# A two-layer encoder trunk: small vectors, turned weights, scores, states and sums of squares put elsewhere

## The chip, the core and the metric

The kernel runs on one core of a Trainium2 chip. Its time is the device time of one execution in microseconds (us). Five engines work side by side, each through its own queue in order: PE (matrix products; its weight loads are listed as PEld), DVE (vector work), ACT (activation functions and copies), POOL (GpSimd) and SP (here it only issues DMAs). PE writes to PSUM, eight banks of 128 x 512 float32; the tags `mm`, `sm`, `lg` and `tp` own two banks each.

## What is computed

Input `x` is 512 tokens by 1024, `mem` 256 tokens by 1024. Cut to what matters:

```python
for i in range(2):
    h = rms_norm(x, attn_norm[i])
    if i == 0:   # differential attention: 6 heads, two softmaxes each, T5 bias
        mix = diff_attention(q, k, v, qk_norm, lambdas, out_norm, rel_bias, lam_init)
    else:        # gated linear attention: 4 heads, chunks of 64
        mix = gla_attention(q, k, v, r, gate_low, gate_w, gate_b, out_norm)
    cross = memory_cross_attention(mem_q, mem, mem_norm[i], w_mem_kv[i], mem_qk_norm[i])
    x = x + concat([mix, cross]) @ w_out[i]
    x = x + conv_ffn(rms_norm(x, ffn_norm[i]), w_up[i], conv_w[i], conv_b[i], w_down[i])

# in gla_attention, per chunk, with eg = exp(cumulated gate), ieg = 1/eg:
a_past   = (q * eg)  @ (k * ieg).T
a_future = (q * ieg) @ (k * eg).T
scores   = where(key <= query, a_past, a_future)
# the state over the chunks: state = decay * state + (k * exp(g_end - g)).T @ v
```

## The kernel before

The residual stream is kept transposed: eight tiles `xT[k]` of 128 channels by 512 tokens. Large products are done in three parts: an operand is split into a rounded high half and a low half (`xh`, `xl`), so are the weights (`whi`, `wlo`), and high times high, high times low and low times high are summed in PSUM. Weights come from memory in pieces (`load_raw`, issued by SP); ACT casts the high half (L199), DVE subtracts for the low half (L200). Splitting an activation is one ACT instruction (L232) and one DVE instruction (L233). The token norm is applied after the product, by a scale per token worked out from sums of squares: `squares` squares a tile on ACT (L332) and adds it to the running sum on DVE (L334); `token_rsqrt` sums over the channels by products with ones (L340).

PE's order is that of the program. The other engines' order is chosen by a scheduler with a model of the times, save in the opening (the block over `ini`), where ACT, DVE, POOL and SP also keep the program's order among the instructions of that block; instructions from outside may be put between them. In the opening the first weight piece and the tiles of x are split, k by k, while PE multiplies them; at k = 4 two rows of biases are made (`bias_rows`, L314 and L315); at k = 6 the second piece is split and the token scale is made. Behind it come loads of constants: `cols` (the norm gains as columns) and `lv` (four lambda vectors). `small_vectors` multiplies seven of these columns by fixed factors (L414 to L417) and works out lambda (L320 to L323).

While a stage waits for softmaxes and the like, PE is given other products from a queue (`Filler`): `fill(us)` takes some us of units from it, `need(name)` takes all up to a mark.

Memory attention (`MemAttn`) goes in slots: `logits` of a block (L484, row maxima on DVE L487, exponentials on ACT L491), `turn` (four transposes into a `tp` bank, L168, copied out by L501), `values` (L513). In layer 0 its slots lie between those of the differential heads (L601 scores, L606 bias and maxima, L637 values) and share the `tp` banks with `prepare` and `finish`.

Gated attention has four heads. `products(h)` makes the scaled q and k, six DVE instructions (L832 to L837). `scores(h)` makes the past scores of two blocks at a time (L843, evicted by a masked copy on DVE, L845, and a copy on ACT, L848), then the future scores of all four (L851, evicted by L852). Each of these three takes one `lg` bank. `states(h, b2)` makes the chunk states (L870); the first is copied by DVE (L873), the others are added to the decayed state (L875).

`update(n, p, gain, acc)` adds a product to `xT[n]` (L946), splits the sum and takes its squares. It is called by the output projection (`out_proj`, tiles of 3 to 6 products of 3 parts each, bank tag `mm`) and by the down-projections of the MLP (`ffn`). The MLP's scale per token is made by `row_scales` (L1002) after the first up-projection.

Of the kernel before, what the change touches and what calls it, by code (L numbers as in the profile page):

```python
# [127 lines left out]
def trunk(ctx, tc, x_t, mem_t, wpack, cols_a_d, cols_d, conv_d, gate_d, rel_bias, diff_lambda, consts, onehot, out):  # L128
# [200 lines left out]

    def squares(src, acc):  # L330
        sq = xtile()
        A.activation(sq, src, AF.Square)  # L332
        if acc[0] is not None:
            V.tensor_add(sq, sq, acc[0])  # L334
        acc[0] = sq

    def token_rsqrt(tag, sq, nb, y, on_dve=False):
        p = bank(tag)
        for b in range(nb):
            mm(p[:, b:b + 1], sq[:, blk(b)], ones[:, 0:1], start=True, stop=True)  # L340
        return rsqrt(p[:, :nb], nb, 1.0 / D, on_dve, y=y)

    E = mybir.EngineType
    load = nc.sync.dma_start
    with tc.tile_pool(name="ini", bufs=1) as ip, tc.manual_schedule(engines={E.Activation, E.DVE, E.Pool, E.SP}):
# [20 lines left out]
        load(oh, onehot)  # L366
        second = [load_raw(raw_tile(), WTILE) for _ in range(3)]
        parts, acc, split_w = [], [None], [None]
        made.append(parts)
# [13 lines left out]
        for k in range(KT):  # L383
            if k + 1 < KT:
                operands(k + 1)
            if k == 0:
                second.append(load_raw(raws[0], WTILE))
            if k == 4:
                bias_rows(rb, oh, bs)
            if k == KT - 2:  # L390
                make_piece(second)
                weights(("qk", 0))
                token_rsqrt("lg", acc[0], NB, r_x[:, 0])
                for c in range(2):
                    load(bias_d[:, 512 * c:min(512 * c + 512, 640)], bs[c])
            hi, lo = parts[k]
            for b in range(NB):
                mm(first[b], xh[k][:, blk(b)], hi, start=k == 0, stop=False)
                mm(first[b], xh[k][:, blk(b)], lo, start=False, stop=False)
                mm(first[b], xl[k][:, blk(b)], hi, start=False, stop=k == KT - 1)  # L400

    load(C[:, 0:640], consts[:, 0:640])
    for i in range(4):
        load(memT[i], mem_t[i])
    load(cols, cols_d)
    load(lv, diff_lambda[0].rearrange("a b -> (a b)").partition_broadcast(128))
    for l in range(2):
        load(cv[l].rearrange("p a b -> p (a b)"), conv_d[l])
    load(gw, gate_d)

    def small_vectors():
        lam(lv, xtile()[:, 0:128].rearrange("p (a b) -> p a b", a=2))
        for c in (c_dq, c_mq(0), c_mq(1)):
            V.tensor_scalar_mul(c, c, 0.125)  # L414
        V.tensor_scalar_mul(c_do, c_do, 1.0 - LAM_INIT)
        for t in range(3):
            V.tensor_scalar_mul(c_go(t), c_go(t), 0.5)  # L417

# [42 lines left out]
    class MemAttn:  # L461
# [33 lines left out]
        def turn(self, u):  # L495
            pe, sm = self.live[u]
            pt = bank("tp")
            for t in range(4):
                transpose(pt[:, blk(t)], pe[:, blk(t)])
            pT = xtile()  # L500
            A.copy(pT, pt)  # L501
            self.live[u] = pT, sm
# [39 lines left out]
    def diff_layer(pool, mix):  # L542
# [117 lines left out]
        norms(0, 1)  # L660
        small_vectors()
        gemm(xh, xl, NB, ("vm", 0), 512, halves(v0, qm))
# [52 lines left out]
    def gla_layer(pool, mix, acc):  # L715
# [106 lines left out]
        def products(h):  # L822
# [7 lines left out]
            x = qx[h] = pool.tile([96, NB, 192], F32, name="qx", bufs=2)  # L830
            x = x.rearrange("p b (c n) -> p b c n", n=64)
            V.tensor_mul(x[:, :, 0:3:2], pq[:96].rearrange("p (b c n) -> p b c n", b=NB, c=2), eg)  # L832
            V.tensor_mul(ki, pk[:96], ie)
            V.tensor_mul(qi, pq[:96], ie)
            V.tensor_mul(x[:, :, 1], x[:, :, 2], eg[:, :, 0, 63:64].to_broadcast([96, NB, 64]))
            V.tensor_mul(ke, pk[:96], egs[h % 2])
            V.tensor_mul(ed, pk[:96], ed)  # L837

        def scores(h):
            for b2 in range(2):  # L840
                pp = bank("lg")
# [6 lines left out]
                A.copy(sv[0:64, 2 * b2:2 * b2 + 2, 64:128], pv[0:64, :, 1])  # L848
            pp = bank("lg")
            for b in range(NB):  # L850
                mm(pp[:, blk(b)], ke[:, blk(b)], qi[:, blk(b)], start=True, stop=True)  # L851
            V.copy_predicated(sv, MF.unsqueeze(1).to_broadcast([128, NB, 128]),  # L852
                              pp.rearrange("p (b n) -> p b n", b=NB))

# [9 lines left out]
        def states(h, b2):  # L864
            if h:
                F.need("v")
            p = bank("lg")
            for b in (0, 1) if b2 == 0 else (2,):
                sl = p[:96, blk(b % 2, 192)]
                mm(sl, kd[h][:, b], v[:, b, blk(h, 192)], start=True, stop=True)  # L870
                sn = pool.tile([96, 192], F32, name="st", bufs=4)
# [72 lines left out]

    def update(n, p, gain, acc):
        V.tensor_add(xT[n], xT[n], p)  # L946
# [3 lines left out]
        split(xh[n], xl[n], xT[n], gain(n))  # L950
        squares(xT[n], acc)

# [7 lines left out]
    def out_proj(l, mix, part, acc):  # L960
        got = {}

        def unit(c, ks, n, i):
# [6 lines left out]
            if i == len(ks) - 1:  # L970
                update(2 * c + n, p, None if acc is None else (lambda k: c_ffn(l, k)), acc)
        todo, kk = tiles(l, part)
# [4 lines left out]
    def ffn(pool, l, acc):  # L977
# [32 lines left out]
        for half, nq in enumerate(HALVES):  # L1010
# [22 lines left out]
            for c in range(4):  # L1033
# [4 lines left out]
                for n in range(2):  # L1038
                    update(2 * c + n, pn[n], (lambda k: c_attn(1, k)) if last and l == 0 else None, acc2)
                    if last and l == 0:  # L1040
# [92 lines left out]
```

## Time and profile before

| | us |
|---|---|
| median of 3 runs | 1227.61 (1224.9 to 1227.72) |
| the profiled execution | 1228.05 |
| its span in the profile | 1226.3 |
| PE busy | 1200.7 (98%) |
| PEld busy | 978.5 (80%) |
| DVE busy | 753.3 (61%) |
| ACT busy | 549.0 (45%) |
| POOL busy | 3.7 (0%) |

A busy time is a sum over the whole span, in which stages have different limits. The list of waits says what ended an engine's idle time; the granted clock is the share of PE's full speed in a window. A line number is that of the kernel before, and may be a helper's.

### The profile page before, as it was taken

How to read it: one execution, taken by the hardware profiler on the slowest of the kernel's cores; microseconds unless marked ns; L12 is line 12 of the kernel's file. 1: busy time of each engine (PE TensorE's matmuls, PEld its weight loads, DVE VectorE, ACT ScalarE, POOL GpSimd, SP SyncE). 2: the span in 40 equal slices, each digit the busy share in tenths (PEclk: the TensorE clock that was granted, in tenths of full speed). 3: DMA queues.
4: the chain of work that ended last, by engine and by line, in shares of the span. 5: the costliest groups of instructions: out<-in, count | busy, mean ns of one | idle time of the engine just before them, and what ended most of it. 6: DMA issues, size and time to landing. Idle time of an engine off the chain costs nothing.

```text
span 1226.3 us, 14737 instructions
## 1 busy us (share of the span) xinstructions
PE 1200.7 (98%) x5678; PEld 978.5 (80%) x5678; DVE 753.3 (61%) x1253; ACT 549.0 (45%) x929; POOL 3.7 (0%) x23
## 2 busy tenths in 40 slices
PE   8999999999999999999999999999999999999998
PEld 6877777778888888888787787887788888888887
DVE  6468566788676533767546345667767662376741
ACT  6566666554443322444436543434544332243420
POOL 0000000000000000000000000000000000000000
PEclk9999998999999999999999999999999999999999
DMA  8233231133132322322341221134223232232231
GB/s 274 84 101 120 78 103 52 53 111 104 69 121 86 121 88 67 115 91 86 116 151 63 69 69 56 40 121 132 100 69 117 90 105 88 83 112 95 84 114 43
DMA packets 39375, 117.73 MB, mean 96 GB/s; under 512 B 4685, under 2 KB 5732, under 8 KB 39306
## 3 DMA queue, kind: packets, MB, share of 16 engines
q1 hardware_dynamic: 39162, 116.79, 29.0%
q8 instruction: 44, 0.72, 0.2%
q14 instruction: 25, 0.20, 0.1%
q10 hardware_dynamic: 144, 0.02, 0.0%
HBM read 112.58 MB, written 4.21 MB: 95 GB/s over the span
## 4 chain that ended last, share of the span: by engine, by line
PE 87%; DVE 5%; ACT 4%; DMA 2%; issue 1%; SPq 0%; ACTq 0%; DVEq 0%
PE ps_mm L266 8%; PE ps_mm L267 8%; PE ps_mm L268 8%; PE ps_sm L266 6%; PE ps_sm L267 6%; PE ps_sm L268 6%; PE ps_mm L249 5%; PE ps_mm L251 5%; PE ps_mm L250 5%; PE ps_tp L266 3%; PE ps_tp L267 3%; PE ps_tp L268 3%; PE ps_lg L267 3%; PE ps_lg L268 3%; PE ps_lg L266 3%; PE ps_tp L168 2%
## 5 line engine op out<-in xcount | busy, mean ns | idle before, releaser
L199 ACT CAST whi<-raw 128x1024 fp32r<-128x1024 f32 (+4 forms) x215 | 208.3, 975 | 250.5 <-PE ps_tp L267 133.6
L200 DVE TENSOR_TENSOR wlo<-raw,whi 128x1024 fp32r<-128x1024 f32 (+4 forms) x215 | 240.2, 1128 | 110.8 <-ACT whi L199 107.2
L266 PE MATMUL ps_mm<-xsh,whi 128*128 128x512 f32 x480 | 191.3, 399 | 2.5 <-DVE xt L946 2.5
L267 PE MATMUL ps_mm<-xsl,whi 128*128 128x512 f32 x480 | 187.5, 391 | 0.1
L268 PE MATMUL ps_mm<-xsh,wlo 128*128 128x512 f32 x480 | 187.6, 391 | 0.0
L249 PE MATMUL ps_mm<-whi,xsh 128*128 128x512 f32 (+2 forms) x352 | 137.9, 392 | 0.1
L266 PE MATMUL ps_sm<-xsh,whi 128*128 128x512 f32 x352 | 136.9, 389 | 0.0
L267 PE MATMUL ps_sm<-xsl,whi 128*128 128x512 f32 x352 | 136.9, 389 | 0.0
L268 PE MATMUL ps_sm<-xsh,wlo 128*128 128x512 f32 x352 | 136.9, 389 | 0.0
L251 PE MATMUL ps_mm<-whi,xsl 128*128 128x512 f32 (+2 forms) x352 | 131.3, 373 | 0.3 <-DVE xsl L233 0.3
L250 PE MATMUL ps_mm<-wlo,xsh 128*128 128x512 f32 (+2 forms) x352 | 130.6, 371 | 0.0
L995 ACT ACTIVATE cvo<-u,cv 128x512 f32<-128x512 f32 x88 | 71.6, 814 | 114.0 <-DVE u L993 113.7
L266 PEld LDWEIGHTS ps_mm<-xsh,whi 128*128 128x128 f32 x480 | 90.4, 188 | 23.3 <-DVE xt L946 2.8
L268 PEld LDWEIGHTS ps_mm<-xsh,wlo 128*128 128x128 f32 x480 | 90.4, 188 | 19.3
L267 PEld LDWEIGHTS ps_mm<-xsl,whi 128*128 128x128 f32 x480 | 90.5, 189 | 18.6 <-DVE xsl L233 0.5
L996 DVE SCALAR_TENSOR_TENSOR cvo<-u,cv,cvo 128x512 f32<-128x512 f32 x88 | 65.9, 749 | 31.7 <-ACT cvo L995 31.5
L249 PEld LDWEIGHTS ps_mm<-whi,xsh 128*128 128x128 f32 x352 | 66.3, 188 | 13.9 <-issue 3.2
L268 PEld LDWEIGHTS ps_sm<-xsh,wlo 128*128 128x128 f32 x352 | 66.1, 188 | 13.8
L266 PEld LDWEIGHTS ps_sm<-xsh,whi 128*128 128x128 f32 x352 | 66.1, 188 | 13.7
L267 PEld LDWEIGHTS ps_sm<-xsl,whi 128*128 128x128 f32 x352 | 66.1, 188 | 13.7
L251 PEld LDWEIGHTS ps_mm<-whi,xsl 128*128 128x128 f32 x352 | 66.1, 188 | 12.7 <-DVE xsl L233 0.5
L250 PEld LDWEIGHTS ps_mm<-wlo,xsh 128*128 128x128 f32 x352 | 66.5, 189 | 9.4
(237 smaller groups left out, 1762.5 us busy)
## 6 DMA issues: line engine op xcount, KB each, us to landing
raw<-in_wpack_dram SPq DMA_DIRECT2D x176, 512.0 KB, 3.5
raw<-in_wpack_dram SPq DMA_DIRECT2D x28, 256.0 KB, 2.6
xt<-in_x_t_dram SPq DMA_DIRECT2D x16, 256.0 KB, 5.4
xres<-xt SPq DMA_DIRECT2D x8, 256.0 KB, 3.0
xt<-xres SPq DMA_DIRECT2D x8, 256.0 KB, 3.6
out_dram<-xt SPq DMA_DIRECT2D x8, 256.0 KB, 2.0
bt<-bias_d SPq DMA_DIRECT2D x6, 256.0 KB, 4.5
raw<-in_wpack_dram SPq DMA_DIRECT2D x4, 384.0 KB, 3.0
```

Of the source, the lines that this page charges most:

```text
L168: nc.tensor.transpose(dst, src, ident[:n, :n])
L199: A.copy(hi[:, c], raw[:, c])
L200: V.tensor_sub(lo[:, c], raw[:, c], hi[:, c].bitcast(F32))
L249: mm(p, sh[k][:, blk(b)], hi, start=k == 0, stop=False)
L250: mm(p, sh[k][:, blk(b)], lo, start=False, stop=False)
L251: mm(p, sl[k][:, blk(b)], hi, start=False, stop=k == KT - 1)
L266: mm(p, hi[:, blk(n)], bh, start=i == first, stop=False)
L267: mm(p, hi[:, blk(n)], bl, start=False, stop=False)
L268: mm(p, lo[:, blk(n)], bh, start=False, stop=i == last)
L995: A.activation(c, u[:, 2:], AF.Identity, scale=cv[l][:, 2, j:j + 1], bias=cv[l][:, 3, j:j + 1])
L996: V.scalar_tensor_tensor(c, u[:, 1:S + 1], cv[l][:, 1, j:j + 1], c, op0=ALU.mult, op1=ALU.add)
```

## The change

- `cols` and `lv` are loaded by SP inside the opening's block, between the third and the fourth weight tile of the second piece. `small_vectors` is called inside the block, after `token_rsqrt`; the seven multiplications come ahead of lambda.
- `MemAttn.turn` copies the turned weights by DVE instead of ACT (16 copies of 128 x 512).
- `scores` makes the future scores first, then the past scores of two blocks, a `fill(1.2)`, and those of the other two. `products` issues its six DVE instructions in another order.
- `states` issues both products of a call ahead of their evictions.
- `squares` can add on GpSimd. The down-projection of layer 0 and the output projection of layer 1 use it, but for the last tile (n = 7).

```diff
-    def squares(src, acc):
+    def squares(src, acc, eng=V):
...
-            V.tensor_add(sq, sq, acc[0])
+            eng.tensor_add(sq, sq, acc[0])
...
+    def small_vectors():
+        for c in (c_dq, c_mq(0), c_mq(1)):
+            V.tensor_scalar_mul(c, c, 0.125)
+        V.tensor_scalar_mul(c_do, c_do, 1.0 - LAM_INIT)
+        for t in range(3):
+            V.tensor_scalar_mul(c_go(t), c_go(t), 0.5)
+        lam(lv, xtile()[:, 0:128].rearrange("p (a b) -> p a b", a=2))
...
         second = [load_raw(raw_tile(), WTILE) for _ in range(3)]
+        load(cols, cols_d)
+        load(lv, diff_lambda[0].rearrange("a b -> (a b)").partition_broadcast(128))
...
                 token_rsqrt("lg", acc[0], NB, r_x[:, 0])
+                small_vectors()
...
-    load(cols, cols_d)
-    load(lv, diff_lambda[0].rearrange("a b -> (a b)").partition_broadcast(128))
...
-            A.copy(pT, pt)
+            V.tensor_copy(pT, pt)
...
         norms(0, 1)
-        small_vectors()
...
+            V.tensor_mul(qi, pq[:96], ie)
             V.tensor_mul(x[:, :, 0:3:2], pq[:96].rearrange("p (b c n) -> p b c n", b=NB, c=2), eg)
+            V.tensor_mul(ke, pk[:96], egs[h % 2])
             V.tensor_mul(ki, pk[:96], ie)
-            V.tensor_mul(qi, pq[:96], ie)
             V.tensor_mul(x[:, :, 1], x[:, :, 2], eg[:, :, 0, 63:64].to_broadcast([96, NB, 64]))
-            V.tensor_mul(ke, pk[:96], egs[h % 2])
             V.tensor_mul(ed, pk[:96], ed)
...
         def scores(h):
+            pp = bank("lg")
+            for b in range(NB):
+                mm(pp[:, blk(b)], ke[:, blk(b)], qi[:, blk(b)], start=True, stop=True)
+            V.copy_predicated(sv, MF..., pp...)
             for b2 in range(2):
...
                 A.copy(sv[0:64, 2 * b2:2 * b2 + 2, 64:128], pv[0:64, :, 1])
-            pp = bank("lg")
-            for b in range(NB):
-                mm(pp[:, blk(b)], ke[:, blk(b)], qi[:, blk(b)], start=True, stop=True)
-            V.copy_predicated(sv, MF..., pp...)
+                if b2 == 0:
+                    F.fill(1.2)
...
-            for b in (0, 1) if b2 == 0 else (2,):
+            bs = (0, 1) if b2 == 0 else (2,)
+            for b in bs:
+                mm(p[:96, blk(b % 2, 192)], kd[h][:, b], v[:, b, blk(h, 192)], start=True, stop=True)
+            for b in bs:
                 sl = p[:96, blk(b % 2, 192)]
-                mm(sl, kd[h][:, b], v[:, b, blk(h, 192)], start=True, stop=True)
...
-    def update(n, p, gain, acc):
+    def update(n, p, gain, acc, eng):
...
-        squares(xT[n], acc)
+        squares(xT[n], acc, V if n == KT - 1 else eng)
...
-                update(2 * c + n, p, None if acc is None else (lambda k: c_ffn(l, k)), acc)
+                update(2 * c + n, p, None if acc is None else (lambda k: c_ffn(l, k)), acc, G if l else V)
...
-                    update(2 * c + n, pn[n], (lambda k: c_attn(1, k)) if last and l == 0 else None, acc2)
+                    update(2 * c + n, pn[n], (lambda k: c_attn(1, k)) if last and l == 0 else None, acc2, G)
```

More of the change, by code (lines that the diff above doesn't have):

```diff
@@ L409, in trunk @@
     load(gw, gate_d)
[L411 to L417, printed above, removed]
     mem_acc = [None]
@@ L831, in products @@
             x = x.rearrange("p b (c n) -> p b c n", n=64)
+            V.tensor_mul(qi, pq[:96], ie)
             V.tensor_mul(x[:, :, 0:3:2], pq[:96].rearrange("p (b c n) -> p b c n", b=NB, c=2), eg)
+            V.tensor_mul(ke, pk[:96], egs[h % 2])
             V.tensor_mul(ki, pk[:96], ie)
-            V.tensor_mul(qi, pq[:96], ie)
             V.tensor_mul(x[:, :, 1], x[:, :, 2], eg[:, :, 0, 63:64].to_broadcast([96, NB, 64]))
-            V.tensor_mul(ke, pk[:96], egs[h % 2])
             V.tensor_mul(ed, pk[:96], ed)
         def scores(h):
+            pp = bank("lg")
+            for b in range(NB):
+                mm(pp[:, blk(b)], ke[:, blk(b)], qi[:, blk(b)], start=True, stop=True)
+            V.copy_predicated(sv, MF.unsqueeze(1).to_broadcast([128, NB, 128]),
+                              pp.rearrange("p (b n) -> p b n", b=NB))
             for b2 in range(2):
@@ L848, in scores @@
                 A.copy(sv[0:64, 2 * b2:2 * b2 + 2, 64:128], pv[0:64, :, 1])
-            pp = bank("lg")
-            for b in range(NB):
-                mm(pp[:, blk(b)], ke[:, blk(b)], qi[:, blk(b)], start=True, stop=True)
-            V.copy_predicated(sv, MF.unsqueeze(1).to_broadcast([128, NB, 128]),
-                              pp.rearrange("p (b n) -> p b n", b=NB))
+                if b2 == 0:
+                    F.fill(1.2)
         def turn_keys(h):
```

## The prediction

> **What bounds the kernel now.** I read the page's busy times first, then the list of who waited for whom for PE (engine, line, releaser: total us, times, longest), then windows around each wait (which give the granted clock), then the timeline there.
>
> ```profile
> span 1226.3 us, 14737 instructions
> PE 1200.7 (98%) x5678; PEld 978.5 (80%) x5678; DVE 753.3 (61%) x1253; ACT 549.0 (45%) x929; POOL 3.7 (0%) x23
> ```
> ```profile
> PE ps_lg L340 <- DVE xt L334: 3.1, 1, 3.1
> PE ps_sm L513 <- ACT xt L501: 3.0, 2, 2.1
> PE ps_mm L266 <- DVE xt L946: 2.5, 5, 0.7
> PE ps_lg L851 <- ACT xt L848: 2.4, 4, 0.8
> PE ps_tp L168 <- ACT xt L501: 2.3, 1, 2.3
> PE ps_lg L870 <- DVE st L873: 2.1, 4, 0.7
> PE ps_lg L601 <- ACT xt L491: 1.6, 4, 0.8
> ```
> ```profile
> 27.60:33.30 5.70, 5.70 (x17) 4.85 (x18) 5.05 (x8) 0.47 (x2) 0.00 (x0) 0.50 0.82 254
> 160.00:240.00 80.00, 75.43 (x453) 59.66 (x450) 57.85 (x161) 49.99 (x140) 0.14 (x1) 0.96 0.23 73
> 197.80:204.30 6.50, 6.48 (x26) 5.39 (x27) 2.87 (x10) 3.59 (x9) 0.00 (x0) 0.50 0.01 3
> 683.80:685.90 2.10, 0.04 (x1) 0.00 (x0) 1.81 (x3) 2.06 (x5) 0.00 (x0) 1.00 0.01 2
> 848.80:863.90 15.10, 13.54 (x58) 10.30 (x57) 15.07 (x22) 11.27 (x16) 0.00 (x0) 1.00 0.40 132
> ```
>
> PE is busy 1200.7 of 1226.3 us, its order is fixed by the program, and the change gives it the same matrix products. So only two things can move the end: the 25.6 us in which PE stands, and work done at a lower clock. The seven waits shown hold 17.0 us of those 25.6. The windows (span, then PE, PEld, DVE, ACT, POOL busy, then the granted clock) show what the list can't: behind the 3.1 us wait PE ran 5.7 us at clock 0.50, and behind the 2.3 us wait 6.5 us at 0.50. Work at half clock costs half its time, so the true prices are 3.13 + 2.85 = 5.98 us and 2.33 + 3.25 = 5.58 us. The 2.1 us stand at 683.8 left the clock at 1.00.
>
> **1. The opening (small vectors and two loads).** Timeline rows (start us, us, engine, line; here and below rows are picked, and those between left out):
>
> ```profile
> 12.57 2.55 SPq L206 DMA_DIRECT2D raw<-in_wpack_dram  x4
> 16.11 0.43 SPq L405 DMA_DIRECT2D cols<-in_cols_dram  x1
> 17.53 1.24 PE L314 MATMUL ps_lg<-oh,rb 32*6 32x512 f32 x4
> 22.52 0.28 DVE L414 TENSOR_SCALAR cols<-cols 128x1 f32<-128x1 f32 x3 [6.41 <-DMA cols<-in_cols_dram]
> 22.95 0.87 DVE L315 COPY xt<-ps_lg 6x512 f32<-6x512 f32 x2
> 24.09 0.39 PE L400 MATMUL ps_sm<-whi,xsl 128*128 128x512 f32 x1
> 24.51 1.05 ACT L199 CAST whi<-raw 128x1024 fp32r<-128x1024 f32 x1 [3.21 <-DVE xsl L233]
> 26.88 0.67 DVE L334 TENSOR_TENSOR xt<-xt 128x512 f32<-128x512 f32 x1
> 27.61 1.87 PE L340 MATMUL ps_lg<-C,xt 128*128 128x1 f32 x8 [3.13 <-DVE xt L334]
> 38.74 1.87 DVE L303 TENSOR_REDUCE ss<-xt 128x8 f32<-128x512 f32 x3 [5.45 <-ACT xt L302]
> ```
>
> The seven multiplications stand outside the hand-ordered block; the scheduler put them on DVE ahead of the bias rows' copies (L315), where they wait 6.41 us for `cols`. Behind them in DVE's queue are L315, the operands of k = 6 and 7, and the last sum of squares (L334), for which PE waits at L340. The change puts them inside the hand-ordered block, behind the token scale: they can't be hoisted. L315 then waits only for PE's L314, which ends at 17.53 + 1.24 = 18.77. From the start of L315 (22.95) to the end of L334 (27.55) the queue takes 4.60 us, so the last sum is ready at 23.4. PE finishes k = 5 at 24.48: 1.1 us of margin, no wait, no clock drop. Gain 5.98, of which I keep 5.9.
>
> What it adds: nothing new is computed. DVE does the seven multiplications (0.68 us in three rows, of which 0.28 is quoted) and the small lambda product after the token scale; that falls into the 5.45 us in which DVE stands before L303, so it costs nothing; without that cover it would delay the q/k norm by about 1.5 us. ACT's one small exponential goes there too, ahead of evictions that wait for PE. On SP, `cols` and `lv` go in front of the fourth weight tile of the second piece: two issues of 0.43. That tile's cast starts at 24.51 and waits for a buffer, not for its data, and nothing says how much slack its data have. Bounds: 0, and all 5.9 us if it comes late by the margin and more. I take 0, since its issue lies some 9 us ahead of the cast. The constants' load behind it is first used by transposes after the next product. `bias_d`'s stores now start 4 us earlier, as do all loads queued behind them. The next thing PE could wait for is the normalised q and k, whose chain starts when PE ends the first product, as before.
>
> **2. Turned weights by DVE (L501, 16 copies).**
>
> ```profile
> 194.40 0.66 PE L168 MATMUL ps_tp<-C,xt 128*128 128x128 f32 x4
> 194.64 1.28 DVE L487 TENSOR_REDUCE nmm<-ps_lg 128x2 f32<-128x512 f32 x2
> 197.18 0.59 ACT L501 COPY xt<-ps_tp 128x512 f32<-128x512 f32 x1
> 655.77 0.67 DVE L771 COPY xt<-ps_tp 16x512 f32<-16x512 f32 x1
> 680.84 1.28 DVE L487 TENSOR_REDUCE nmm<-ps_lg 128x2 f32<-128x512 f32 x2
> 684.00 1.22 DVE L200 TENSOR_TENSOR wlo<-raw,whi 128x1024 fp32r<-128x1024 f32 x1 [1.88 <-ACT whi L199]
> 685.25 0.60 ACT L501 COPY xt<-ps_tp 128x512 f32<-128x512 f32 x1
> 691.84 1.28 DVE L487 TENSOR_REDUCE nmm<-ps_lg 128x2 f32<-128x512 f32 x2
> 695.01 1.10 PE L513 MATMUL ps_sm<-vm,xt 128*128 128x64 f32 x8 [0.91 <-ACT xt L501]
> ```
>
> ACT's 0.59 us becomes 0.67 on DVE (L771 reads the same width from the same bank); the duration matters little, the queue it stands in does. On ACT the copy is queued behind four exponentials, which wait for DVE's row maxima. Layer 0: the transposes end at 195.06, the maxima at 195.92; DVE then copies until 196.6, and PE's next transposes, which need the bank, start there instead of 197.82. The stand shrinks from 2.33 to about 1.1 us: gain 1.2. Whether the clock still drops can't be read directly; the nearest row is the 2.1 us stand at 683.8 that kept 1.00, so I take no drop: gain 3.2 more, together 4.4 (bounds 0 and 5.6). Layer 1: at 682.12 DVE has its maxima done and stands until 684.00, when the next low half (L200) gets its cast; the copy fits there and PE's stand (2.1 us) goes. The second (0.9 us) goes likewise: maxima done at 693.12, copy at 693.8, PE there at 695.01 - 0.91 = 694.1. Gain 3.0 (bounds 0 and 3.0: if the scheduler puts the copy behind L200, it ends at 685.9, as before).
>
> Cost: DVE gets 8 x 0.67 = 5.4 us in 160 to 240 us, where it is busy 57.85 of 80; ACT loses 4.7. There DVE also frees PE's output banks (L946) and adds the bias for the heads' scores; a copy ahead of these delays them by up to 0.67. Bounds 0 and 5.4, less what the exponentials gain (L601 waits 1.6 us for them now); I take 1.0.
>
> [...]
>
> **3. Scores reordered (4 heads).** L851 asks for a third bank of a pair and waits for the first pair's evictions (L845, then ACT's L848): 2.4 us, four times 0.6. After the change the masked future scores go first into bank A, the first past pair into bank B, then 1.2 us of filler, then the second past pair needs A back, which takes DVE's one eviction:
>
> ```profile
> 729.00 1.46 PE L843 MATMUL ps_lg<-qx,xt 96*128 96x192 f32 x8
> 732.38 0.73 DVE L852 COPY_PREDICATED xt<-C,ps_lg 128x512 f32<-128x512 int32 x1 [1.45 <-PE ps_lg L851]
> ```
>
> The first past pair takes 0.73 us (L843's 1.46 for both) and the filler 1.2: 1.9 us against 0.73 plus at most one low half of 1.22 in front. That covers it nearly; gain 2.4 less 0.4 = 2.0 (bounds 0 and 2.4). The filler is work PE has to do anyway; 4.8 us are taken from later fills, which by the costs in the code still reach the end of the layer. In `products` the operands change their order: the future product needs its third of six, at about 1.8 us, before 2.5 us of filler and more have passed. It costs nothing while this filler lasts, 0.6 us a head without it.
>
> **4. States reordered.** Both products go in before DVE's first eviction, so PE no longer waits in the middle for DVE to leave the bank: gain 2.1, the whole L870 row. The first state comes some 0.5 us later; PE asks for it after 2.5 us of filler. Next to be late would be nothing on PE.
>
> **5. Sums of squares on GpSimd (6 adds in layer 0's last down-projection, 6 in layer 1's output projection).** In the first, updates are over 5 us apart and nobody waits: 0. In the second, 848.8 to 863.9, DVE is busy 15.07 of 15.10 us, and PE waits for L946 for 1.6 of its 2.5 us:
>
> ```profile
> L334 DVE TENSOR_TENSOR xt<-xt 128x512 f32<-128x512 f32 x7 | 4.8, 685 | 0.0
> L233 DVE SCALAR_TENSOR_TENSOR xsl<-xt,cols,xsh 128x512 fp32r<-128x512 f32 x6 | 4.5, 747 | 0.0
> L946 DVE TENSOR_TENSOR xt<-xt,ps_mm 128x512 f32<-128x512 f32 x6 | 3.8, 680 | 0.0
> L200 DVE TENSOR_TENSOR wlo<-raw,whi 128x1024 fp32r<-128x1024 f32 x3 | 3.7, 1223 | 0.0
> ```
> ```profile
> 615.71 0.52 POOL L766 MEMSET xt<- 17x512 f32 x1 [358.10 <-DMA xres<-xt]
> ```
>
> Six of seven L334 leave DVE: 6 x 0.69 = 4.1 us, after which PE (13.54 us busy) is the slower. Gain at most 1.6. No add by GpSimd is in the trace; its nearest row is a fill of the same width, 0.52 us. A tile comes every 2.1 us here, so an add up to four such fills keeps pace. Whether it slows DVE the trace can't tell; if each add held DVE for three fills (1.6 us), DVE would lose 9.4 to save 4.1, and about 3.5 us of that would reach PE. Bounds -3.5 and +1.6; I take two fills with part of it beside L946: +0.8. The last add stays on DVE, so the final scale isn't put behind GpSimd.
>
> [...]
>
> **The sum.** 5.9 + 4.4 + 3.0 - 1.0 + 2.0 + 2.1 + 0.8 = 17.2. The profiled execution took 1228.05 us (span 1226.3 and 1.75 around it), 0.4 above the median 1227.61 of the runs: 1210.9, so 1211.
>
> **Rivals.**
> (a) The clock drops in layer 0's memory attention all the same: 3.2 back, 1214. For it: 1.1 us of standing come right after transposes, and the trace has drops after 2.33 and 3.13. Against: 2.1 us kept it.
> (b) DVE's copies queue behind low halves, or hold up L946 and the heads' scores: part 2 brings nothing, 7.4 less and 1.0 more, about 1219. For it: 72% busy DVE at 160 to 240; against: at 682.12 and 693.12 DVE stands.
> (c) The opening keeps a wait, because the displaced weight tile is late or another outside instruction is hoisted (the change then doesn't do what it says): 5.9 back, 1217. Against: the margins above.
> (d) Slower: GpSimd's adds are a chain, and the row scales of layer 1's MLP need it. If one add took x us, the last would end 6x after the first square; PE asks just behind the window of 15.1 us, some 16 us after it. Lost are 6x - 16 us. To undo 17.2 and 3.7 more, x must pass 6.2 us, twelve times the fill of 0.52. At that price 1232. Nothing in the trace comes near it.
>
> **How the numbers follow.** Forecast 1211: 0.55; (a) 0.17; (b) 0.13; (c) 0.10; (d) 0.05. The forecast's own terms reach from 1206 (all bounds on the good side, without the waits for L491) to 1216. The range 1206 to 1220 takes in (a), (b) and (c) and leaves out (d) and their mixtures. A difference under 0.3% (3.7 us) can't be told from none: slower 0.05, (d); same 0.05, taken from (b) and (c) where they meet the bad end of part 5; faster 0.90.
>
> **What would show it.** Right: no L340 wait near 24 us and clock 1.00 from 20 to 40; L315 on DVE near 18.8; no wait for L501's successor at 684 and 694 us; clock 1.00 from 160 to 240; no waits at the future scores and the states; DVE under 90% busy in the output projection of layer 1. Wrong: DVE instructions of 1.5 us and more beside GpSimd's adds, new PE waits on DVE copies between 160 and 240, or clock 0.50 anywhere behind the opening.

## The result: 1207.02 us, and the profile after

The changed kernel takes 1207.02 us in the median of 4 runs (1206.70 to 1207.84); the kernel before, beside it on the same chip, 1226.26 us in 4 runs (1224.63 to 1227.72). The ratio is 0.9844, with a 95% interval from 0.9827 to 0.9862. The forecast was 1211 us (1206 to 1220). The profiled execution after took 1206.70 us with a span of 1204.9; before it was 1228.05 and 1226.3, so the two traces differ by 21.4 us, and this is what is explained here.

The page of the kernel after, its busy times, and then its list of who waited for whom for PE (line numbers are 1 to 4 higher than before, so L501 is now L502 and L946 is L950; the scores changed places):

```profile
span 1204.9 us, 14764 instructions
PE 1191.4 (99%) x5678; PEld 974.2 (81%) x5678; DVE 758.8 (63%) x1257; ACT 539.7 (45%) x913; POOL 22.9 (2%) x35
```
```profile
PE ps_mm L266 <- DVE xt L950: 2.0, 3, 1.0
...
PE ps_tp L168 <- DVE xt L502: 1.1, 1, 1.1
...
PE ps_sm L514 <- DVE xt L502: 0.8, 1, 0.8
```

PE now stands for 13.5 us instead of 25.6, and is busy for 9.3 us less with the same 5678 products: the one is waits; of the other some 6 us are work that no longer runs at half clock, half of 5.7 and 6.5 us. The waits at the bias sum (L340), the scores and the states are gone from the list. Windows of the kernel after (span, then PE, PEld, DVE, ACT, POOL busy, then the granted clock, DMA share, GB/s):

```profile
20.00:40.00 20.00, 20.00 (x94) 16.65 (x93) 15.30 (x37) 10.27 (x24) 0.29 (x2) 1.00 0.68 226
160.00:240.00 80.00, 77.05 (x480) 61.79 (x478) 67.24 (x179) 47.95 (x134) 0.14 (x1) 1.00 0.27 87
826.80:843.20 16.40, 15.36 (x68) 12.15 (x66) 15.85 (x18) 12.01 (x18) 11.01 (x6) 1.00 0.32 102
```

The clock is 1.00 in the opening and in layer 0's attention, where it was 0.50 for 5.7 and 6.5 us; in the opening of before, products of 128 x 512 start 0.43 us apart at 0.50 (from 29.91 on) and 0.23 us apart behind it (from 33.97 on). DVE does more in 160 to 240 (67.24 us, 57.85 before) and PE still gains there. In the last window, layer 1's output projection, DVE is as full as before. Rows of the timeline of the kernel after (start, us, engine, line, and in brackets the idle time before it and what ended it), from the opening, layer 0's memory attention, layer 1's, and the gated attention:

```profile
17.85 0.88 DVE L315 COPY xt<-ps_lg 6x512 f32<-6x512 f32 x2 [1.49 <-PE ps_lg L314]
...
21.78 0.67 DVE L334 TENSOR_TENSOR xt<-xt 128x512 f32<-128x512 f32 x1
...
23.57 0.95 PE L340 MATMUL ps_lg<-C,xt 128*128 128x1 f32 x8
...
23.77 1.05 ACT L199 CAST whi<-raw 128x1024 fp32r<-128x1024 f32 x1 [2.71 <-PE ps_sm L411]
```
```profile
187.68 1.28 DVE L488 TENSOR_REDUCE nmm<-ps_lg 128x2 f32<-128x512 f32 x2
...
188.88 0.68 DVE L502 COPY xt<-ps_tp 128x512 f32<-128x512 f32 x1
...
189.61 0.66 PE L168 MATMUL ps_tp<-C,ks 128*128 128x128 f32 x4 [1.08 <-DVE xt L502]
...
670.40 0.68 DVE L502 COPY xt<-ps_tp 128x512 f32<-128x512 f32 x1
...
675.72 1.10 PE L514 MATMUL ps_sm<-vm,xt 128*128 128x64 f32 x8 [0.84 <-DVE xt L502]
```

The small multiplications have left the place in front of L315 (they run from 28.11 on, as L345): the last sum of squares is ready at 22.45, PE asks for it at 23.57 and doesn't stand. The copy of turned weights (L502) follows the row maxima at once in layer 0, and PE stands for 1.08 us there, not 2.33. In layer 1 the two stands of before (2.07 and 0.91 us) are both gone, and a new one of 0.84 us has come between them, at a copy that PE did not wait for before.

To see where the 21.4 us come from, the table takes five instructions that PE executes in every kernel and gives their start, minus the start in the profile of before, in us: the first product of q and k (36.94 before), the token sum of layer 1 (642.26), the first transposes of q in the gated attention (725.36), those of its last `finish` (839.35), and the products of the row scale behind layer 1's output projection (865.33). The difference of two neighbours is what a stage gained. The start of PE itself wanders: its bias product L314 begins between 16.79 us (after) and 17.89 us (states alone) in these profiles, 17.53 in that of before, so differences of some tenths, and up to 1 us, in the first column mean nothing. The -1.49 and -1.27 there are for the most part the clock (last section).

| kernel | q and k | sum, layer 1 | gated, first | gated, last | row scale | span |
|---|---|---|---|---|---|---|
| after | -6.97 | -11.61 | -14.19 | -19.96 | -21.39 | -21.4 |
| opening alone | -6.81 | -8.20 | -8.13 | -8.03 | -8.03 | -8.1 |
| turned weights alone | +0.18 | -4.47 | -7.03 | -7.04 | -7.02 | -7.1 |
| scores alone | -1.49 | -4.40 | -4.34 | -6.56 | -7.18 | -7.2 |
| states alone | +0.26 | -1.19 | -0.26 | -3.28 | -3.28 | -3.3 |
| squares alone | -1.27 | -1.24 | +1.14 | +1.19 | +0.37 | +0.4 |
| after, squares on DVE | -6.77 | -11.36 | -13.64 | -19.40 | -20.02 | -20.0 |
| after, half the squares on DVE | -5.99 | -10.62 | -13.18 | -18.94 | -20.75 | -20.3 |

### The profile page after: what moved, and what is told of

Its sections match the earlier page's. It is cut to its first block, busy times and chain, and to the rows that moved or that the text cites. A ratio compares the mean times of both kernels' runs of the same rounds, so it can differ in the third digit from the quotient of the medians.

```text
span 1204.9 us, 14764 instructions
## 1 busy us (share of the span) xinstructions
PE 1191.4 (99%) x5678; PEld 974.2 (81%) x5678; DVE 758.8 (63%) x1257; ACT 539.7 (45%) x913; POOL 22.9 (2%) x35
## 4 chain that ended last, share of the span: by engine, by line
PE 92%; DVE 4%; ACT 2%; issue 1%; DMA 1%; ACTq 0%; DVEq 0%
PE ps_mm L266 8%; PE ps_mm L267 8%; PE ps_mm L268 8%; PE ps_sm L266 6%; PE ps_sm L267 6%; PE ps_sm L268 6%; PE ps_mm L249 6%; PE ps_mm L251 6%; PE ps_mm L250 6%; PE ps_tp L266 3%; PE ps_tp L267 3%; PE ps_tp L268 3%; PE ps_lg L267 3%; PE ps_lg L268 3%; PE ps_lg L266 3%; PE ps_tp L168 2%
## 5 line engine op out<-in xcount | busy, mean ns | idle before, releaser
L200 DVE TENSOR_TENSOR wlo<-raw,whi 128x1024 fp32r<-128x1024 f32 (+4 forms) x215 | 241.5, 1133 | 110.4 <-ACT whi L199 109.4
L266 PE MATMUL ps_mm<-xsh,whi 128*128 128x512 f32 x480 | 190.7, 397 | 2.0 <-DVE xt L950 2.0
L267 PE MATMUL ps_mm<-xsl,whi 128*128 128x512 f32 x480 | 187.1, 390 | 0.1
L268 PE MATMUL ps_mm<-xsh,wlo 128*128 128x512 f32 x480 | 187.1, 390 | 0.0
L266 PE MATMUL ps_sm<-xsh,whi 128*128 128x512 f32 x352 | 136.9, 389 | 0.0
L267 PE MATMUL ps_sm<-xsl,whi 128*128 128x512 f32 x352 | 136.9, 389 | 0.0
L268 PE MATMUL ps_sm<-xsh,wlo 128*128 128x512 f32 x352 | 136.9, 389 | 0.0
L266 PEld LDWEIGHTS ps_mm<-xsh,whi 128*128 128x128 f32 x480 | 90.2, 188 | 22.2 <-DVE xt L950 2.4
L268 PEld LDWEIGHTS ps_mm<-xsh,wlo 128*128 128x128 f32 x480 | 90.1, 188 | 19.1
L267 PEld LDWEIGHTS ps_mm<-xsl,whi 128*128 128x128 f32 x480 | 90.2, 188 | 18.8 <-DVE xsl L233 0.8
L268 PEld LDWEIGHTS ps_sm<-xsh,wlo 128*128 128x128 f32 x352 | 66.1, 188 | 13.8
L266 PEld LDWEIGHTS ps_sm<-xsh,whi 128*128 128x128 f32 x352 | 66.1, 188 | 13.7
L267 PEld LDWEIGHTS ps_sm<-xsl,whi 128*128 128x128 f32 x352 | 66.1, 188 | 13.6
```

Of the source, the lines that this page charges most:

```text
L200: V.tensor_sub(lo[:, c], raw[:, c], hi[:, c].bitcast(F32))
L266: mm(p, hi[:, blk(n)], bh, start=i == first, stop=False)
L267: mm(p, hi[:, blk(n)], bl, start=False, stop=False)
L268: mm(p, lo[:, blk(n)], bh, start=False, stop=i == last)
```

## The experiments

Five do one part of the change alone in the kernel before, and a sixth does half of a part there; the other five change the kernel after. Where two kernels differ by less than about 0.3% (the 4 runs of before beside the result lie 3.1 us apart), they are told apart by the stages of their profiles, not by their times.

**The opening alone.**

```diff
+        load(cols, cols_d)      # behind the third weight tile
+        load(lv, ...)
...
                 token_rsqrt("lg", acc[0], NB, r_x[:, 0])
+                small_vectors()
```

> The kernel before with part 1 of the change alone. Theory (PE stood for the sum of squares because DVE waited for cols, and the clock fell behind it): no L340 wait near 24 us, clock 1.00 from 20 to 40 us, the first L249 near 30 us instead of 36.94, about 6 to 7 us less: 1219 to 1221 against 1226. Rival (the clock is low there for another reason, such as the start or the loads): only the wait goes, 3.1 us less, and clock 0.50 stays in the window behind it.

1219.68 us (1219.12 to 1220.02) against 1226.52, ratio 0.9943 (0.9930 to 0.9956). From its timeline:

```profile
23.74 0.95 PE L340 MATMUL ps_lg<-C,xt 128*128 128x1 f32 x8
```

No idle time stands in front of it. The stage gained 6.81 us in the profiles (0.57 of it because PE began earlier), and the medians differ by 6.84. Without the earlier start it is 6.24 us, a little over what the prediction took for the stand and the clock drop behind it (5.9), and nothing of the displaced loads shows.

**Only the loads of the opening moved, in the kernel before.** The multiplications stay outside the block.

```diff
+        load(cols, cols_d)
+        load(lv, ...)
...
-    load(cols, cols_d)
-    load(lv, ...)
```

> The kernel before with only the two loads moved into the opening's block; the small vectors stay outside it, where the scheduler now puts the seven multiplications ahead of k = 1's operands on DVE, since its model has cols there sooner. Theory (what counts is the fixed place on DVE, not the earlier load): DVE stands from about 6.5 us until cols has landed near 20 us, PE runs dry at k = 1 and ends the first product 6 to 10 us later: 1232 to 1237. Rival (the earlier load is what gained): the wait for cols shrinks by the 1.6 us by which the load is issued earlier, 1.6 us less than before or better.

1235.37 us (1235.00 to 1238.32) against 1227.75, ratio 1.0075 (1.0060 to 1.0090): slower by 7.6 us. Its timeline:

```profile
20.39 0.28 DVE L414 TENSOR_SCALAR cols<-cols 128x1 f32<-128x1 f32 x3 [14.27 <-DMA cols<-in_cols_dram]
...
22.22 0.79 PE L401 MATMUL ps_mm<-wlo,xsh 128*128 128x512 f32 x1 [13.02 <-DVE wlo L200]
```

The multiplication starts 2.1 us earlier than before (20.39 against 22.52), but with the load ahead in the program it stands much further forward on DVE, ahead of operands of k = 1. DVE waits for `cols` for 14.27 us with these behind it, and PE for 13.02 us, against about 6 that the old stand and its clock had cost. So the earlier load by itself gains nothing; with the fixed place behind the token scale the opening gains. The fixed place without the earlier loads was not run; that it alone would do is argued from before, where `cols` had landed by 22.52, well ahead of 28.11, where the multiplications now run. The run also shows how much hangs on where the scheduler drops an instruction that no loop holds.

**Turned weights alone.**

```diff
-            A.copy(pT, pt)
+            V.tensor_copy(pT, pt)
```

> The kernel before with the turned weights copied by DVE alone. Theory (the copy stood behind ACT's exponentials): layer 0's stand falls from 2.33 to 1.1 us, the clock stays at 1.00 there, layer 1's 3.0 us of waits fall to about 0.8; 6.5 to 7.5 us less against a run of before in which the clock falls, some 4 us less against one in which it doesn't. Rival (DVE becomes the late one): L946 and L601 waits grow by as much, gain under 3 us.

1220.61 us (1219.11 to 1221.03) against 1226.52, ratio 0.9950 (0.9938 to 0.9961). Layer 0's stage gained 4.65 us in the profiles and layer 1's 2.56, the same as in the kernel after (4.64 and 2.58). A row of its list of waits for PE, and a window around the stand, which is 1.08 us at 196.75 here:

```profile
PE ps_lg L601 <- ACT xt L491: 0.8, 3, 0.3
```
```profile
189.00:209.00 20.00, 18.92 (x133) 15.51 (x134) 15.12 (x48) 12.62 (x38) 0.00 (x0) 1.00 0.12 40
```

Layer 0 by rows: 1.25 us of stand and 0.8 that the scores no longer wait for the exponentials (L601 by L491: 1.6 before). For the clock the prediction took 3.2 to 3.25, half of the time at half speed. The table has a measurement: with the scores alone nothing in layer 0 is changed, the clock stayed at 1.00 behind the same stand (last section), and the stage was 2.9 us shorter. 1.25, 0.8 and 2.9 make 4.95, the stage gained 4.65, so some 0.3 us are left that DVE's longer queue may have cost.

**Scores alone, and states alone.**

```diff
+            pp = bank("lg")                    # scores: the future pair first
...
+                if b2 == 0:
+                    F.fill(1.2)
```
```diff
+            for b in bs:                       # states: both products ahead of the evictions
+                mm(p[:96, blk(b % 2, 192)], kd[h][:, b], v[:, b, blk(h, 192)], ...)
```

> The kernel before with the reordered scores and products and the fill of 1.2 alone. Theory: the four L851 waits (2.4 us) go and nothing takes their place: 2 to 3 us less, 0.2%. Rival (the second past pair waits for bank A, or the filler is missing later): waits of 0.6 a head come back at the second past pair or at the end of the layer, under 1 us.

> The kernel before with both state products issued ahead of their evictions, alone. Theory: the four L870 waits (2.1 us) go, 2 to 3 us less, 0.2%. Rival (the first state comes late for the outputs): a wait of 0.5 a head at L887, no gain.

Scores: 1222.14 us (1220.24 to 1224.17) against 1226.52, ratio 0.9964 (0.9951 to 0.9977). States: 1224.65 us (1220.73 to 1225.39), ratio 0.9978 (0.9969 to 0.9988). These two ratios mislead, as runs of kernels that keep ACT's copies spread by several us with the clock (last section); the stage tells more (the columns to its left hold nothing that these kernels change). The gated attention gained 2.22 us by the scores and 3.02 by the states, and with the scores the output projection behind it is 0.62 shorter. That is the same work in another place: between the two marks PE runs 34 products of L266, 34 of L267 and 34 of L268 before, and 33 of each with the scores alone, since the `fill(1.2)` takes units from later fills and runs them in the gated attention. So the scores are worth 2.84 us. One row of the list of waits of the kernel with the scores alone:

```profile
PE ps_lg L872 <- DVE st L875: 2.6, 4, 1.3
```

Before, this wait at the states was 2.1 us. With the scores alone, half a microsecond of what they gain is lost again there; with both edits it isn't, and the stage gained 5.77 us, 0.53 more than the two alone.

**Sums of squares alone, and the kernel after without them.**

```diff
-            V.tensor_add(sq, sq, acc[0])
+            eng.tensor_add(sq, sq, acc[0])
```
```diff
-                update(2 * c + n, p, ..., acc, G if l else V)
+                update(2 * c + n, p, ..., acc, V)
...
-                    update(2 * c + n, pn[n], ..., acc2, G)
+                    update(2 * c + n, pn[n], ..., acc2, V)
```

> The kernel before with the sums of squares on GpSimd alone. Theory (in layer 1's output projection GpSimd's adds and DVE's instructions with two SBUF inputs hold each other up): DVE's L233 and L200 there grow by some 0.4 us each, of the 1.6 us of L946 waits about half is left: 0.5 to 1 us less, hardly to be measured. Rival (DVE is simply relieved): L946 waits gone, 1.6 us less.

> The changed kernel with all sums of squares back on DVE. Theory: L946's successor waits 1.6 us again in layer 1's output projection against 1.0 with GpSimd, so 0.3 to 1 us more than the changed kernel: about 1207.5. Rival (GpSimd's adds cost more than they save): 0.5 us or more less than the changed kernel.

Alone: 1226.93 us (1222.86 to 1228.56) against 1226.68, ratio 0.9998 (0.9988 to 1.0007). The kernel after without this part: 1208.20 us (1207.93 to 1208.97), ratio 0.9850 (0.9837 to 0.9862). Neither time tells this part from nothing. The stage of the output projection does, and agrees both ways: 0.82 us gained alone, and 1.43 against 0.62 in the kernel after. How it comes about is another matter. DVE's groups in 826.8 to 843.2, first of the kernel after (adds on GpSimd), then of the kernel after without this part (busy us, mean ns | idle time before):

```profile
L233 DVE SCALAR_TENSOR_TENSOR xsl<-xt,cols,xsh 128x512 fp32r<-128x512 f32 x7 | 7.6, 1080 | 0.0
L200 DVE TENSOR_TENSOR wlo<-raw,whi 128x1024 fp32r<-128x1024 f32 x4 | 6.0, 1491 | 0.2 <-ACT whi L199 0.2
L950 DVE TENSOR_TENSOR xt<-xt,ps_mm 128x512 f32<-128x512 f32 x6 | 4.1, 679 | 0.3 <-PE ps_mm L268 0.3
```
```profile
L233 DVE SCALAR_TENSOR_TENSOR xsl<-xt,cols,xsh 128x512 fp32r<-128x512 f32 x7 | 5.2, 749 | 0.0
L200 DVE TENSOR_TENSOR wlo<-raw,whi 128x1024 fp32r<-128x1024 f32 x4 | 4.9, 1223 | 0.0
L334 DVE TENSOR_TENSOR xt<-xt 128x512 f32<-128x512 f32 x7 | 4.8, 688 | 0.0
```

DVE gave away 4.1 us of adds (six of seven L334) and got 3.5 back: L233 became longer by 2.4 us, L200 by 1.1. The adds on GpSimd, from the timeline of the kernel after:

```profile
831.11 7.43 POOL L334 TENSOR_TENSOR xt<-xt 128x512 f32<-128x512 f32 x4 [1.93 <-ACT xt L332]
```

These four adds took 1.61 to 2.14 us each (the 7.43 us run from the start of the first to the end of the last); the shortest of the twelve in the kernel took 1.29, the longest 2.27. In the same timeline the long instructions of DVE are those that begin while such an add is under way: L233 takes 1.16 to 1.77 us then (four times) and L200 2.31 (once), and with no add under way at their start 0.74 to 0.75 and 1.21 to 1.23. L950, which has one of its inputs in PSUM where those two have none, takes 0.68 to 0.69 in the five that begin beside an add, and 0.67 without one. Its mean is 679 ns in the kernel after and 683 in the one without this part. Rows of that timeline:

```profile
827.61 1.57 POOL L334 TENSOR_TENSOR xt<-xt 128x512 f32<-128x512 f32 x1 [7.31 <-ACT xt L332]
827.95 0.68 DVE L950 TENSOR_TENSOR xt<-xt,ps_mm 128x512 f32<-128x512 f32 x1
...
829.86 1.23 DVE L200 TENSOR_TENSOR wlo<-raw,whi 128x1024 fp32r<-128x1024 f32 x1 [0.21 <-ACT whi L199]
...
831.01 0.74 DVE L233 SCALAR_TENSOR_TENSOR xsl<-xt,cols,xsh 128x512 fp32r<-128x512 f32 x1
...
833.98 1.20 DVE L233 SCALAR_TENSOR_TENSOR xsl<-xt,cols,xsh 128x512 fp32r<-128x512 f32 x1
...
835.10 2.31 DVE L200 TENSOR_TENSOR wlo<-raw,whi 128x1024 fp32r<-128x1024 f32 x1
```

**Half the adds back on DVE.** In layer 1 only tiles 1, 3 and 5 stay on GpSimd.

```diff
-        squares(xT[n], acc, V if n == KT - 1 else eng)
+        squares(xT[n], acc, V if n == KT - 1 or (l == 1 and n % 2 == 0) else eng)
```

> The changed kernel with GpSimd adding only the squares of tiles 1, 3 and 5 in layer 1's output projection, DVE the others (layer 0 as changed). Theory (GpSimd's adds and DVE's two-input instructions hold each other up, so half the adds give the better part of the relief): waits of L946's successor there fall from 1.0 us to under 0.5, 0.3 to 0.7 us less than the changed kernel's stage. Rival (DVE's own work is what counts): waits rise to between 1.0 and 1.6, 0.3 us more.

1206.87 us (1206.80 to 1207.80) against 1227.75, ratio 0.9839 (0.9825 to 0.9854). It can't be told from the kernel after by time. In the stage it gained 1.81 us against 1.43 (L266's wait for L946's successor is 0.6 us there, 1.0 in the kernel after), and DVE's instructions are back at their old length:

```profile
L233 DVE SCALAR_TENSOR_TENSOR xsl<-xt,cols,xsh 128x512 fp32r<-128x512 f32 x8 | 6.0, 748 | 0.0
L200 DVE TENSOR_TENSOR wlo<-raw,whi 128x1024 fp32r<-128x1024 f32 x4 | 4.9, 1223 | 0.4 <-ACT whi L199 0.4
```

So three adds take load off DVE without making its instructions longer. In this trace each of the three runs 1.54 to 1.67 us and starts while an L233 is under way that ends after its usual 0.75 us; whether that order is what spares DVE, no run shows. The 0.4 us are below what the time of the whole kernel can show.

**A stand brought back into the opening: four and seven idle adds on DVE.** They stand behind the bias rows and delay the last sum of squares.

```diff
                 bias_rows(rb, oh, bs)
+                for _ in range(4):             # or 7
+                    V.tensor_add(dmy, idle, idle)
```

> The changed kernel with 4 additions of 128x512 put on DVE behind the bias rows in the opening (their result isn't used). They take 4 x 0.6 = 2.4 us; with 1.1 us of margin PE stands about 1.3 us at L340. Theory (a short stand doesn't lower the clock): 1.3 us more than the changed kernel, clock 1.00. Rival (any stand there does): about 4 us more, clock 0.50 for 5 to 6 us behind it.

> The same with 7 additions: 4.2 us, PE stands about 3.1 us at L340, as in the kernel before, though no load is waited for. Theory (the length of the stand lowers the clock): clock 0.50 for 5 to 6 us behind it, 6 us more than the changed kernel. Rival (the clock fell for another reason): 3.1 us more, clock 1.00.

Four adds: 1214.69 us (1212.58 to 1215.07), ratio 0.9898 (0.9885 to 0.9911), 7.7 us more than the kernel after. Seven adds: 1212.89 us (1212.41 to 1214.17), ratio 0.9888 (0.9873 to 0.9902), 5.9 more. Four adds cost no less than seven; the ranges overlap, and in the profiles PE reaches the token sum of layer 1 1.30 us later with four (638.65 us, 637.35 with seven). Timeline and windows of the kernel with four:

```profile
25.98 1.13 PE L340 MATMUL ps_lg<-C,xt 128*128 128x1 f32 x8 [1.56 <-DVE xt L334]
...
34.25 1.04 ACT L199 CAST whi<-raw 128x1024 fp32r<-128x1024 f32 x1 [3.17 <-PE ps_sm L414]
...
36.18 0.50 PE L249 MATMUL ps_mm<-whi,xsh 128*128 128x512 f32 x1 [1.97 <-ACT ks L558]
```
```profile
26.00:28.00 2.00, 2.00 (x11) 1.81 (x12) 2.00 (x2) 0.00 (x0) 0.00 (x0) 0.71 0.04 8
28.00:30.00 2.00, 2.00 (x6) 1.62 (x5) 2.00 (x3) 0.00 (x0) 0.00 (x0) 0.50 0.84 256
30.00:32.00 2.00, 2.00 (x9) 1.58 (x9) 1.37 (x12) 0.47 (x2) 0.00 (x0) 0.94 0.87 279
```

The planned stand of 1.56 us is followed by some 3.4 us at half clock (0.29, 0.50 and 0.06 of full speed missing in three windows of 2 us: 1.7 us of work lost). Besides, the scheduler now puts a cast ahead of the evictions of q and k on ACT; the cast itself waits 3.17 us for PE, so the evictions start only at 35.30, though the token scale that they need was ready at 31.67. PE stands for another 1.97 us up to 36.18, and the clock drops again (0.79 over the 8 us behind). So a stand well under 2 us can lower the clock: the theory of this run failed, and the drop of its rival came, but for 3.4 us and not 5 to 6. With seven adds the stand is 3.74 us and ends at 27.77, and no second stand follows:

```profile
27.00:35.00 8.00, 7.22 (x25) 6.16 (x26) 6.73 (x19) 0.63 (x3) 0.00 (x0) 0.63 0.55 184
```

A clock of 0.63 over these 8 us is 5.9 us at half speed, up to about 32.9, of which PE works 5.1 behind the stand. 3.74 and half of 5.1 make 6.3; in the profile, this kernel's PE is 6.67 us behind the kernel after when it begins q and k, 0.30 of it because L314 began later.

**The turn ahead of the logits.** To take away the 1.08 us that is left in layer 0.

```diff
+            if 0 <= t - 1 < 8:
+                self.turn(t - 1)
             if t in (0, 2, 4, 6):
                 self.logits(t // 2)
-            if 0 <= t - 1 < 8:
-                self.turn(t - 1)
```

> The changed kernel with a slot's turn issued ahead of its logits, so that DVE's copy goes ahead of the row maxima. Theory (the two stands left behind the copies, 1.08 us in layer 0 and 0.84 us in layer 1, come from the copy's place behind two maxima of 0.6 us): both go, 1.5 to 2 us less than the changed kernel. Rival (the exponentials, now later by 0.68, hold up the next scores): waits of L602 grow by as much, no gain.

1215.10 us (1213.26 to 1215.82) against 1227.75, ratio 0.9902 (0.9887 to 0.9918): 8 us slower than the kernel after. The wait at L168 is gone and a larger one is in its place; from the list of waits and a window:

```profile
PE ps_lg L602 <- ACT xt L492: 4.7, 6, 2.5
```
```profile
160.00:240.00 80.00, 74.33 (x436) 58.51 (x435) 62.08 (x169) 44.96 (x127) 0.14 (x1) 0.94 0.23 77
```

The row maxima come later, so the exponentials do, and the heads' scores wait for the banks these read; the rival's wait is there, only much longer than 0.68 us. In layer 1 the stand isn't gone either (1.1 us, 0.8 in the kernel after); there the copy stands behind a low half and not behind the maxima. The clock drops twice, behind the 2.5 us wait and again behind two short ones (timeline, and a window behind them):

```profile
195.17 0.48 PE L602 MATMUL ps_lg<-kT,qT 64*128 64x128 f32 x2 [0.95 <-ACT xt L492]
196.08 1.00 PE L602 MATMUL ps_lg<-kT,qT 64*128 64x128 f32 x6 [0.43 <-ACT xt L492]
```
```profile
196.36:199.36 3.00, 3.00 (x16) 2.68 (x15) 1.09 (x5) 1.91 (x6) 0.00 (x0) 0.50 0.02 5
```

The 1.08 us are the price of an order in which nothing worse is late.

## Why the prediction was right, and where its terms were off

The sum was 17.2 us and the traces differ by 21.4. By the table:

| term | predicted | measured |
|---|---|---|
| opening | 5.9 | 6.97, of it 0.74 an earlier start of PE |
| layer 0's attention | 4.4 - 1.0 | 4.64 |
| layer 1's memory attention | 3.0 | 2.58 |
| scores | 2.0 | 2.84 (2.22 + 0.62) |
| states | 2.1 | 3.02 |
| both of these together, beyond each alone | 0 | 0.53 |
| squares | 0.8 | 0.81 |

**Opening: right in cause and size.** The window from which the price of the clock was read ends at 33.30; in the trace the clock is 0.50 for 0.42 us more, so the price was 6.2 and not 5.98, and 6.97 less 0.74 is 6.23. L315 was forecast near 18.8 and ran at 17.85, since PE's L314 began at 16.79. The displaced weight tile was issued at 18.66, 5.1 us ahead of its cast and not 9, and the cast waited for PE all the same (2.71 us, `PE ps_sm L411`). Rival (c) fell, but the loads moved alone show that it was a real danger.

**Turned weights: right, with two terms off.** The stand left in layer 0 was forecast at 1.1 and is 1.08. The cost of 1.0 for DVE's longer queue came out as some 0.3, with 0.8 gained at the scores, so it was no cost on balance. The clock's 3.2 was nearer 2.9. In layer 1 both stands went as forecast; the step that failed is that no other copy was followed into DVE's queue. The copy between the two kept nobody waiting on ACT before. On DVE it meets a low half of 1.22 us and waits behind it, and PE stands for 0.84 us at L514 (timelines of before and after):

```profile
687.50 0.59 ACT L501 COPY xt<-ps_tp 128x512 f32<-128x512 f32 x1 [1.64 <-PE ps_tp L168]
```
```profile
673.84 1.22 DVE L200 TENSOR_TENSOR wlo<-raw,whi 128x1024 fp32r<-128x1024 f32 x1
674.98 0.68 DVE L502 COPY xt<-ps_tp 128x512 f32<-128x512 f32 x1
```

That is rival (b), for one of sixteen copies.

**The clock: the right outcome by an argument that doesn't hold.** The prediction took "no drop" from a stand of 2.1 us at 683.8 that kept the clock at 1.00. The same stand dropped it in other executions (last section), and the four idle adds brought a drop after 1.56 us, so that row was no bound. What is shown is weaker: after a stand of 1.08 us in layer 0 the clock stayed at 1.00 (180 to 210 us) in four profiles: the kernel after, the turned weights alone, and the two with fewer adds on GpSimd. With the turn ahead of the logits, 0.95 and 0.43 us in short order were enough for a drop. So as far as its argument goes the prediction was lucky here, and rival (a) was nearer than its 0.17.

**Scores and states: right in cause, each too small.** The prediction priced the states by their row in the list of waits, 2.1 us. The stage gained 3.02. Timeline of before, and of the states alone:

```profile
737.91 0.49 PE L870 MATMUL ps_lg<-gv,kd 128*96 128x192 f32 x2
738.85 0.24 PEld L870 LDWEIGHTS ps_lg<-gv,kd 128*96 128x96 f32 x2 [0.77 <-DVE st L873]
738.85 0.57 PE L870 MATMUL ps_lg<-gv,kd 128*96 128x192 f32 x2 [0.45 <-DVE st L873]
739.12 0.53 PE L249 MATMUL ps_mm<-whi,xsh 128*128 128x512 f32 x1
```
```profile
737.66 0.81 PE L870 MATMUL ps_lg<-gv,kd 128*96 128x192 f32 x4
738.17 0.53 PE L249 MATMUL ps_mm<-whi,xsh 128*128 128x512 f32 x1
```

From the first state product to the filler behind them PE takes 1.2 us before and 0.5 with the states alone. That is 0.7 us less in three heads and 0.95 in the fourth, 3.0 together, where the list has three waits of 0.45 and one of 0.72. So these waits cost more than the idle time that is listed for them: the products on both sides take 0.49 and 0.57 us here, 0.81 for all four without the wait, and the weight load, idle for 0.77 us, begins together with its product (738.85) and not ahead of it. For the scores, the 0.4 held back for an imperfect cover was not needed, and the waits of 2.4 us were worth 2.84; that the reason is the same was not looked into.

**Squares: the number was right, its working was not.** 0.8 was taken as part of 1.6 us because an add would be short: two fills, the author's estimate from a fill of 0.52 us. The adds take 1.29 to 2.27 us, they stretch DVE's instructions by 3.5 of the 4.1 us saved, and DVE is 97% busy there (15.85 of 16.40), where under 90% was forecast. What is left of the gain is 0.8. Rival (d) needed 6.2 us an add and fell by a wide margin.

## What to carry to other kernels

An instruction outside a hand-ordered block belongs to the scheduler, and one that waits for a load can stand in front of the work that bounds the kernel; give it a fixed place, and don't count on an earlier load to mend it. When PE is 98% busy, look for its few stands in the list of waits and then for the clock behind each of them: here two stands of 5.5 us cost some 11.4 in the profile of before (6.2 and 5.2). Moving a short copy to a fuller engine can gain (4.64 and 2.58 us in two stages here), if what stands ahead of it in that queue is ready sooner; follow every copy there, and not only those that PE waits for now.

## What the runs showed of the hardware that was not expected

**One stand, three prices.** Six profiles hold layer 0's stand of 2.33 us unchanged: those of before, of four single parts, and of the loads moved alone. The 8 us behind it are not the same. The windows, each from the end of the stand, with the opening alone, the scores alone, and the states alone; before it is 0.59, with the squares alone 0.58, with the loads alone 0.79:

```profile
191.01:199.01 8.00, 8.00 (x45) 6.68 (x45) 4.53 (x16) 5.25 (x16) 0.00 (x0) 0.79 0.01 2
```
```profile
196.34:204.34 8.00, 8.00 (x57) 6.60 (x58) 6.10 (x22) 5.71 (x16) 0.00 (x0) 1.00 0.01 2
```
```profile
198.08:206.08 8.00, 8.00 (x45) 6.64 (x45) 4.54 (x17) 5.20 (x16) 0.00 (x0) 0.79 0.01 2
```

Clocks of 0.59, 0.79 and 1.00 over 8 us are some 6.6, 3.4 and 0 us at half speed: by this count 3.3, 1.7 or no us lost. The opening's stand does it too, and not by its length: over the 8 us behind it the clock is 0.62 before (3.13 us of stand) and 0.79 with the scores alone (3.58 us) and the squares alone (3.68 us). The stand of 2.07 us in layer 1, on which the prediction leaned, does the same. Windows of before and of the states alone, which is the same program up to there:

```profile
680.00:690.00 10.00, 7.93 (x52) 6.39 (x50) 5.08 (x7) 6.00 (x15) 0.53 (x1) 1.00 0.46 150
```
```profile
680.00:690.00 10.00, 7.93 (x38) 6.53 (x36) 3.89 (x6) 6.24 (x15) 0.53 (x1) 0.83 0.50 158
```

In the table, this is the second column of the opening alone, the scores alone and the states alone (1.4, 2.9 and 1.4 us gained in layer 0 where nothing was changed) and the third of the states and the squares alone (0.9 and 2.4 us lost, and by the squares no work there is touched). So one profiled execution prices a stand's clock for itself only. It also fits the spread of the kernel before: a run with a mean clock of 0.999 took 1223.5 us, one with 0.994 1228.1. The profile of before had the largest of these prices in layer 0, which is part of why the traces differ by 21.4 us and the medians by 19.2. The kernel after, with shorter stands, spread by 1.1 us.

Where the danger begins stays open. A stand of 1.56 us was enough for a drop (four idle adds), and so were 0.95 and 0.43 us close together (the turn ahead of the logits), while 2.33 us left the clock at 1.00 with the scores alone. Neither the length of a stand nor its place decides it in these traces.
